# Delta rule of a two-block network: heads 2 and 3 with swapped chunk halves, 64-column blocks, passes of two head groups in turn

## The chip, the cores and the metric

The kernel runs on one core of one Trainium2 chip. The metric is the device time of one execution in microseconds (us), median of the runs shown. One core has TensorE (PE in the rows; PEld is its weight load), VectorE (DVE), ScalarE (ACT), GpSimd (POOL) and DMA queues that are issued from SyncE (SP) or from the other engines. TensorE multiplies a stationary operand (the weights, loaded by a LDWEIGHTS) with a moving one and writes to PSUM, which has eight banks of 128 partitions x 512 numbers in fp32.

## The reference

Two blocks of two layers each work on a sequence of 512 tokens of width 1024. The change lies in the second block's gated delta rule: four heads, key and value width 128, chunks of 64 tokens (eight chunks). Cut to what matters:

```
q, k, v, beta, g = chunk(q), chunk(k), chunk(v), chunk(beta), chunk(g)   # chunks of C = 64
g = cumsum(g)
decay = exp(where(tril, g_i - g_j, -inf))
A = where(strict, (k*beta) @ k.T * decay, 0)
T = inverse of (A + eye)                       # unit lower triangular, 64x64 for each chunk and head
u = T @ (v*beta);  w = T @ (k*beta*exp(g))
qk = (q @ k.T) * decay
for each chunk:                                # state S is 128x128 for each head
    v_new = u - w @ S
    o = (q*exp(g)) @ S + qk @ v_new
    S = S*exp(g_last) + (k*exp(g_last - g)).T @ v_new
```

Around it stand the input projections, a causal convolution of width 4 with silu over q, k, v, a dilated attention of eight heads, and the output projection. o is normalised and gated with silu(z).

## The kernel before

One program for the core. All projections are written as three fp32r matmuls for each k tile (`mm3`, lines 179 to 181: high x high, low x high, high x low parts), 512 columns wide; these are most of TensorE's work and serve as filler between the steps of everything else. A scheduler puts the instructions of all parts in one order for each engine by priority; `merges()` stands in a block of higher priority. Work in fp32 runs as two passes for each matmul, each pass a weight load and a stream.

The function `mix2` holds the delta rule. Tokens stand as four tiles of 128 rows (t = 0 to 3), each two chunks of 64 (u = 0, 1). The steps, with their lines:

- z, beta and gates (L915 to L955), the convolution and silu (`conv_silu`, L957 to L970), `k_rows` (transposes of k and its norms).
- Decays and scores for each head: `gB` by matmuls with 128 columns (L1011), `G` = k k.T (L1020), exps for each 128 columns (L1022, L1027), `A` (L1023). Each 128x128 tile holds two chunks, of which the off-diagonal quarters are masked to zero.
- The diagonal 16x16 blocks of A go through DRAM (`dA`), are solved on DVE and go back (`dT`). `q_rows` makes q k.T (L1060).
- `merges()`: for each head the inverse is merged from 16 to 32 to 64 rows: transposes (L274, tile `ps_d`), A x TT (L1120), a copy to X on ACT (L1122), T x X (L1125), a subtraction on DVE (L1126); then u (L1129), w (L1137), copies on ACT. The four heads follow one another in a pipeline.
- The scan, eight steps: `pv` = w S (L1151), `vn` = u + pv on DVE (L1152), `qv` = q S (L1154), `dS` = k.T vn (L1160), the new S on DVE (L1161). pv and qv fill 64 rows of their bank, dS reads 64 rows. After two steps `po` = qk vn (L1167) and the output's norm (L1164 to L1178).
- Attention (L1184 on): casts of its operands into the tiles of A, qT, kN and ET once these are free (L1189 to L1193), scores (L1219, L1220; tile `ps_s`), flips (`ps_pt`), values (L1237, `ps_o`), `delta_out` (flips of o, tile `ps_po`), and the projection (`ps_mo`).

PSUM banks are dealt by role (`deal`): a role with one bank waits until the former tile of that bank has been read.

Of the kernel before, what the change touches and what calls it, by code (L numbers as in the profile page):

```python
# [17 lines left out]
P = 128  # L18
# [19 lines left out]
def shape_consts():  # L38
# [5 lines left out]
    for d in (3, 2, 1, 0):  # L44
# [10 lines left out]
    m16 = (i // 32 == j // 32) & (i % 32 >= 16) & (j % 32 < 16)  # L55
    m32 = same & (i % 64 >= 32) & (j % 64 < 32)
# [3 lines left out]
        "mask_ls": np.where(same & (i > j), 0.0, NEG),  # L60
        "mask_u": np.where(same & (i <= j), 0.0, NEG),
# [29 lines left out]
def body(ctx, tc, a, out, plan, n1=LAYERS, n2=LAYERS, dbg=None):  # L91
# [759 lines left out]
    def rng2(i):  # L851
        return np.arange(o2[i], o2[i + 1])

    def z_w(l, j):
        return take_n("w_in_2", l, np.concatenate([rng2(6)[j * 256:j * 256 + 256], rng2(7 + j)]), range(KT))

    def block2(xt, xd, pss):
        with ExitStack() as c2:
# [15 lines left out]
            dA = [dr.tile([P, 4, SEQ], F32, name=f"dA{l}", bufs=1) for l in range(LAYERS)]  # L874
            dT = [dr.tile([P, 4, SEQ], F32, name=f"dT{l}", bufs=1) for l in range(LAYERS)]
            zt = tmp()
            nc.gpsimd.memset(zt, 0.0)
            for l in range(n2):
                for h in range(4):
                    nc.sync.dma_start(dT[l][:, h], zt)  # L880
# [5 lines left out]
    def mix2(l, rt, xt, par, row, dA, dT, pss):  # L886
# [3 lines left out]
        with ExitStack() as cm:  # L890
            pm = pool(f"pm{l}", cm)
            deal(mm=(0, 1, 2), tr=(3,), d=(4, 5, 6, 7), pv=(4,), qv=(5,), dS=(6,), po=(7,),
# [18 lines left out]

            d_gain, a_log, dt_b = row[:, 0:128], row[:, 128:132], row[:, 132:136]
# [7 lines left out]
            for j in range(2):  # L920
                def ev(t, ps, j=j):
                    zs = z[t][:, tsl(j, 256)]
                    silu2(ps[:, :256], zs, 256)
                    nc.vector.scalar_tensor_tensor(heads(zs, 2), heads(zs, 2), 0.5, mid(d_gain, 2), ALU.mult, ALU.mult)
                    nc.vector.tensor_copy((bb, aa)[j][:, :, t], ps[:, 256:260])
# [20 lines left out]
            nc.vector.tensor_tensor(graw, sp, end(ea, NT), ALU.mult)  # L946
            ps = bank("d")
            nc.tensor.matmul(ps[:, 0:16], cc("tri"), f16(graw), start=True, stop=True)
            nc.tensor.matmul(ps[:, 16:32], cc("same"), f16(graw), start=True, stop=True)
            gc, ngc, kd, eg = s16("gc"), s16("ngc"), s16("kd"), s16("eg")  # L950
            nc.vector.tensor_copy(f16(gc), ps[:, 0:16])
            nc.vector.tensor_scalar(f16(ngc), ps[:, 0:16], -1.0, None, ALU.mult)
            nc.vector.tensor_tensor(f16(kd), ps[:, 16:32], f16(gc), ALU.subtract)
            nc.scalar.activation(kd, kd, AF.Exp)
            nc.scalar.activation(eg, gc, AF.Exp)  # L955


            def conv_silu(m, ps, dst):
                with tc.high_priority(offset=0):
                    conv_silu_(m, ps, dst)  # L960

# [485 lines left out]
```

## Time and profile before

| | us |
|---|---|
| median of 3 runs | 2142.76 (2141.4 to 2145.73) |
| the profiled execution | 2143.14 |
| its span, first to last instruction | 2141.4 |
| around the span | 1.7 |
| TensorE busy in the span | 2059.3 (96%) |
| VectorE busy | 1261.0 (59%) |
| ScalarE busy | 959.2 (45%) |

A busy time is the sum over the records of an engine, and TensorE's passes overlap in their records, so a share of 96% doesn't say that the array is at its peak. The granted clock is 0.994 over the span. In layer 1 of the second block, the stretch 735 to 830 us holds decays, scores and the projections of q and v, 830 to 872 the merges, 872 to 916 the scan, 916 to 941 projections alone, 941 to 1012 the attention. Layer 2 repeats this at 1420 to 1760 us.

### The profile page before, as it was taken

The page shows a single profiled execution, that of the slowest core. Times are in us where ns is not written, and L with a number is a line of the kernel's source. Part 1 is how long each engine was busy: PE and PEld are TensorE (multiplying, and loading weights), DVE is VectorE, ACT ScalarE, POOL GpSimd, SP SyncE. Part 2 cuts the span into 40 slices and gives each one's busy share as a digit, 9 for nine tenths or more (in the row PEclk, how much of TensorE's full clock was granted, in tenths as well). Part 3 has the DMA queues.
Part 4 walks back from the last instruction along what each step waited for, and adds up shares of the span by engine and source line. Part 5 has one row for each costly group of instructions (what it writes and reads, how often), then busy time and mean ns, then how long its engine had stood idle before and what let it go on. Part 6 is the DMA issues. An engine that isn't in the chain of part 4 may idle for free.

```text
span 2141.4 us, 28239 instructions
## 1 busy us (share of the span) xinstructions
PE 2059.3 (96%) x10824; PEld 1709.0 (80%) x10824; DVE 1261.0 (59%) x2106; ACT 959.2 (45%) x1805; POOL 195.5 (9%) x337
## 2 busy tenths in 40 slices
PE   7899999999998899999999999999999999999998
PEld 6687878777887788778788888878887778888886
DVE  5667655667845676663666425577757446662364
ACT  4735444644534553255544324346333644442342
POOL 1110001110001111200200000021112010000001
PEclk9999999999999999999999999999999999999999
DMA  5232133322132522131533333243212144333332
GB/s 169 84 92 69 70 109 118 103 85 91 54 124 84 182 84 59 43 94 50 179 116 93 96 99 99 69 151 121 73 52 60 45 133 152 94 94 98 99 98 89
DMA packets 73717, 207.30 MB, mean 97 GB/s; under 512 B 16560, under 2 KB 17584, under 8 KB 73328
## 3 DMA queue, kind: packets, MB, share of 16 engines
q1 hardware_dynamic: 62576, 200.80, 30.3%
q10 hardware_dynamic: 11008, 4.72, 0.9%
q8 instruction: 85, 1.39, 0.3%
q14 instruction: 48, 0.39, 0.1%
HBM read 182.16 MB, written 17.04 MB: 93 GB/s over the span
## 4 chain that ended last, share of the span: by engine, by line
PE 76%; DVE 7%; ACT 6%; DMA 5%; issue 4%; POOL 3%; POOLq 0%; ACTq 0%; SPq 0%; DVEq 0%
PE ps_mm L180 18%; PE ps_mm L181 18%; PE ps_mm L179 18%; DMA wr<-in_w 4%; DVE wl L144 2%; PE ps_tr L274 2%; PE ps_o L1237 2%; ACT wh L143 2%; PE ps_pt L274 1%; PE ps_mo L181 1%; PE ps_mo L179 1%; PE ps_mo L180 1%; PE ps_s L1220 1%; POOL r2h L297 1%; ACT xn L296 1%
## 5 line engine op out<-in xcount | busy, mean ns | idle before, releaser
L144 DVE TENSOR_TENSOR wl<-wr,wh 128x1024 fp32r<-128x1024 f32 (+4 forms) x304 | 360.7, 1189 | 392.5 <-ACT wh L143 391.2
L143 ACT CAST wh<-wr 128x1024 fp32r<-128x1024 f32 (+4 forms) x304 | 309.3, 1019 | 354.7 <-PE ps_mm L181 151.2
L180 PE MATMUL ps_mm<-wl,xh 128*128 128x512 f32 (+2 forms) x736 | 283.4, 386 | 8.6 <-DVE wl L144 8.6
L181 PE MATMUL ps_mm<-x2h,wl 128*128 128x512 f32 (+1 forms) x768 | 285.9, 372 | 0.0
L179 PE MATMUL ps_mm<-x2h,wh 128*128 128x512 f32 (+1 forms) x768 | 285.7, 372 | 0.0
L180 PE MATMUL ps_mm<-x2l,wh 128*128 128x512 f32 (+1 forms) x768 | 285.7, 372 | 0.0
L179 PE MATMUL ps_mm<-wh,xh 128*128 128x512 f32 (+2 forms) x736 | 283.5, 387 | 1.9 <-ACT wh L143 1.8
L181 PE MATMUL ps_mm<-wh,xl 128*128 128x512 f32 (+2 forms) x736 | 281.7, 384 | 0.0
L180 PEld LDWEIGHTS ps_mm<-wl,xh 128*128 128x128 f32 x736 | 140.3, 191 | 37.2 <-DVE wl L144 14.8
L180 PEld LDWEIGHTS ps_mm<-x2l,wh 128*128 128x128 f32 x768 | 144.8, 189 | 25.0
L179 PEld LDWEIGHTS ps_mm<-x2h,wh 128*128 128x128 f32 x768 | 144.7, 188 | 24.9
L181 PEld LDWEIGHTS ps_mm<-x2h,wl 128*128 128x128 f32 x768 | 144.8, 188 | 24.8
L179 PEld LDWEIGHTS ps_mm<-wh,xh 128*128 128x128 f32 x736 | 139.8, 190 | 28.4 <-ACT wh L143 4.6
L181 PEld LDWEIGHTS ps_mm<-wh,xl 128*128 128x128 f32 x736 | 140.2, 191 | 23.3 <-issue 0.7
L1331 DVE SCALAR_TENSOR_TENSOR rt<-ps_mm,par,rt 128x511 f32<-128x511 f32 (+1 forms) x176 | 131.3, 746 | 4.8 <-ACT rt L1328 1.8
L179 PE MATMUL ps_mm<-xh,wh 128*128 128x512 f32 x320 | 128.0, 400 | 0.9 <-DVE rp L358 0.9
L181 PE MATMUL ps_mm<-xh,wl 128*128 128x512 f32 x320 | 127.1, 397 | 0.0
L180 PE MATMUL ps_mm<-xl,wh 128*128 128x512 f32 x320 | 127.0, 397 | 0.0
L297 POOL TENSOR_SCALAR r2h<-ss 128x1 f32<-128x1 f32 x48 | 19.4, 404 | 996.7 <-ACT th L296 759.8
L179 PE MATMUL ps_mm<-wh,hh 128*128 128x512 f32 x224 | 88.6, 397 | 0.3 <-ACT wh L143 0.2
L180 PE MATMUL ps_mm<-wl,hh 128*128 128x512 f32 x224 | 88.6, 397 | 0.1
L181 PE MATMUL ps_mm<-wh,hl 128*128 128x512 f32 x224 | 88.5, 397 | 0.0
(403 smaller groups left out, 3826.9 us busy)
## 6 DMA issues: line engine op xcount, KB each, us to landing
wr<-in_w SPq DMA_DIRECT2D x270, 512.0 KB, 3.6
gain<-in_gain SPq DMA_DIRECT2D x13, 512.0 KB, 6.4
wr<-in_w SPq DMA_DIRECT2D x14, 384.0 KB, 3.0
x<-in_x SPq DMA_DIRECT2D x8, 512.0 KB, 6.0
wm<-gqk SPq DMA_DIRECT2D x32, 128.0 KB, 2.4
xd<-x SPq DMA_DIRECT2D x8, 512.0 KB, 2.6
xs<-xd SPq DMA_DIRECT2D x8, 512.0 KB, 4.1
xs<-xm SPq DMA_DIRECT2D x8, 512.0 KB, 4.6
```

The source lines that it names most:

```text
L143: nc.scalar.copy(hi[:, :n], raw[:, :n])
L144: nc.vector.tensor_tensor(lo[:, :n], raw[:, :n], hi[:, :n].bitcast(F32), ALU.subtract)
L179: nc.tensor.matmul(ps, l[0], r[0], start=start, stop=False)
L180: nc.tensor.matmul(ps, l[0], r[1], start=False, stop=False)
L181: nc.tensor.matmul(ps, l[1], r[0], start=False, stop=stop)
L274: nc.tensor.transpose(ps[:w, tsl(j)], src[:, tsl(j, w)], ident)
L296: nc.scalar.activation(junk[i], halves[i], AF.Square, accum_out=ss[:, i:i + 1])
L297: nc.gpsimd.tensor_scalar(r[:, i:i + 1], ss[:, i:i + 1], 1.0 / D, r[:, 0:1] if i else EPS, ALU.mult, ALU.add)
L1220: nc.tensor.matmul(o_s, q_[own], kl[own, h // 2, :w], start=False, stop=True)
L1237: nc.tensor.matmul(o[:, tsl(h, 64)], p_[:, tsl(i * (qt + 1) + j)], av[:, j, tsl(h, 64)], start=j == 0, stop=j == qt)
L1331: nc.vector.scalar_tensor_tensor(acc[:, j:], ps[:, :SEQ - j], par[:, w0 + 3 * m + 2 - j:w0 + 3 * m + 3 - j], acc[:, j:], ALU.mult, ALU.add)
```

## The change

Heads 0 and 1 (group 0) stay as they are. Heads 2 and 3 (group 1) hold each pair of chunks in swapped halves: z, beta, the gates and the silu's results are written with chunk u in half 1 - u, and `delta_out` swaps back. So at one step of the scan group 0 works in one half of the partitions and group 1 in the other. Line numbers of the changed kernel are those of its own file.

- Decays (`M`, L1058 and L1060), scores (`G`, L1071) and q k.T (L1110) are made as 64x64 blocks, alternating between the two column halves of TensorE; A and E hold two heads in one 128x512 tile, so the exps and products go by 512 columns.
- The 16x16 blocks are written to DRAM twice, plain and transposed (`dT[0]`, `dT[1]`: 32 DMAs in place of 16 over both layers), which replaces the first transposes; `dA` is written by 4 DMAs in place of 8.
- The merges work on two heads at once, with 64x64 matmuls over 64 rows that alternate between the quadrants (0,0) and (64,64) and write to two banks (L1183, L1186); u (L1196) in the same quadrants, w (L1200) in row halves; transposes (L1179) with 64 rows.
- The scan issues the passes of the two groups in turn: pv and qv (both L1241) in alternating column halves, dS (L1253) in alternating row halves and two banks; vn and S are updated in two pieces of 256 columns. The norm of tile t - 1 (`delta_norm`, po at L1220) is issued after the first step of tile t. `vn` has three buffers.
- dS takes banks 6 and 7, and po moves to bank 3, which `tr` and the attention's `o` use as well.

Matmuls on TensorE over both layers: L1011's 32 become 128; L1020's and L1060's 32 each become 64 each; L1120's and L1125's 128 become 256; u's and w's 32 each become 64 each; transposes 64 become 32; eight small ones (L982) come in; 184 of pv, qv and dS stay 184.

The core of the diff:

```diff
-            deal(mm=(0, 1, 2), tr=(3,), d=(4, 5, 6, 7), pv=(4,), qv=(5,), dS=(6,), po=(7,),
+            deal(mm=(0, 1, 2), tr=(3,), d=(4, 5, 6, 7), pv=(4,), qv=(5,), dS=(6, 7), po=(3,),
                  s=(0, 1, 4), pt=(2, 5), o=(3,), mo=(6, 7))
...
+            F, B = slice(0, 64), slice(64, 128)
+            HF = (F, B)
...
+                if m % 4 < 2:
+                    nc.vector.scalar_tensor_tensor(dst, th, 1.0, acc, ALU.add, ALU.mult)
+                else:
+                    for u in range(2):
+                        nc.vector.scalar_tensor_tensor(chunks(dst)[:, :, 1 - u], chunks(th)[:, :, u], 1.0,
+                                                       chunks(acc)[:, :, u], ALU.add, ALU.mult)
...
+            tri = cc("tri")
+            for g in range(2):
+                M = bank("d")
+                for i in range(8):
+                    h, t, o = 2 * g + i // NT, i % NT, M[:, tsl(i, 64)]
+                    for p in HF:
+                        nc.tensor.matmul(o[p], ngraw[:, h, t:t + 1].to_broadcast([P, 64]), tri[:, p], start=True, stop=False)
+                    for p in HF:
+                        nc.tensor.matmul(o[p], tri[:, p], graw[:, h, t:t + 1].to_broadcast([P, 64]), start=False, stop=True)
                 d = dt()
+                nc.vector.tensor_tensor(b64(d), b64(M), mid(cc("mask_ls"), 8), ALU.add)
+                nc.vector.scalar_tensor_tensor(b64(E[:, g]), b64(M), -1.0, mid(cc("mask_u"), 8), ALU.mult, ALU.add)
                 flush()
+                nc.scalar.activation(d, d, AF.Exp)
+                nc.scalar.activation(E[:, g], E[:, g], AF.Exp)
                 G = bank("d")
+                for i in range(8):
+                    for p in HF:
+                        kc = chunks(kT[2 * g + i // NT])[:, i % NT, HF.index(p)]
+                        nc.tensor.matmul(G[p, tsl(i, 64)], kc, kc, start=True, stop=True)
+                nc.vector.tensor_tensor(d, d, G, ALU.mult)
+                nc.vector.tensor_tensor(b64(A[:, g]), b64(d), end(f16(sa[:, 2 * g:2 * g + 2]), 64), ALU.mult)
+                nc.scalar.dma_start(dA[:, 2 * g:2 * g + 2], A[:, g].rearrange("p (h c) -> p h c", h=2))
...
+            nc.vector.tensor_copy(Lb, Rb.rearrange("p r c -> p c r"))
             for u in range(8):
-                nc.scalar.dma_start(diag(dT, u), Rb[16 * u:16 * u + 16])
+                nc.scalar.dma_start(diag(dT[0], u), Rb[16 * u:16 * u + 16])
+                nc.scalar.dma_start(diag(dT[1], u), Lb[16 * u:16 * u + 16])
...
-                ps = bank("tr")
+                ps = bank("tr")[:, :256]
                 for t in range(NT):
-                    nc.tensor.matmul(ps[:, tsl(t)], kT[h][:, tsl(t)], qT[h][:, tsl(t)], start=True, stop=True)
-                nc.vector.tensor_tensor(ET[h], ps, ET[h], ALU.mult)
+                    for u, p in enumerate(HF):
+                        nc.tensor.matmul(ps[p, tsl(t, 64)], chunks(kT[h])[:, t, u], chunks(qT[h])[:, t, u],
+                                         start=True, stop=True)
...
+            def halves(f):
+                ps = bank("d"), bank("d")
+                for i in range(8):
+                    for p, b in zip(HF, ps):
+                        f(i, p, b)
+                return tuple(zip(HF, ps))
...
+                    T, TT = dt(), dt()
+                    for x, d in ((T, dT[0]), (TT, dT[1])):
+                        nc.scalar.dma_start(x.rearrange("p (h c) -> p h c", h=2), d[:, 2 * g:2 * g + 2])
+                    As = dt(), dt()
+                    for A_, m in zip(As, ("m16", "m32")):
+                        nc.gpsimd.tensor_tensor(b64(A_), b64(A[:, g]), mid(cc(m), 8), ALU.mult)
+                    for A_ in As:
+                        if A_ is As[1]:
+                            for j in range(2):
+                                ps = bank("d")
+                                for t in range(NT):
+                                    nc.tensor.transpose(ps[F, tsl(t)], TT[:, tsl(NT * j + t, 64)], ident)
+                                for u, p in enumerate(HF):
+                                    nc.scalar.copy(b64(T[p, tsl(j, 256)]), chunks(ps[F])[:, :, u])
+                        X = dt()
+                        for p, ps in halves(lambda i, p, b: nc.tensor.matmul(
+                                b[p, tsl(i, 64)], A_[p, tsl(i, 64)], TT[p, tsl(i, 64)], start=True, stop=True)):
+                            nc.scalar.copy(X[p], ps[p])
+                        for p, ps in halves(lambda i, p, b: nc.tensor.matmul(
+                                b[p, tsl(i, 64)], T[p, tsl(i, 64)], X[p, tsl(i, 64)], start=True, stop=True)):
+                            nc.vector.tensor_tensor(TT[p], TT[p], ps[p], ALU.subtract)
+                    Tk = dt()
+                    nc.vector.tensor_tensor(b64(Tk), b64(TT), end(f16(sk[:, 2 * g:2 * g + 2]), 64), ALU.mult)
+                    for j in range(2):
+                        h = 2 * g + j
+                        ps = bank("d"), bank("d")
                         for t in range(NT):
+                            for p, b in zip(HF, ps):
+                                nc.tensor.matmul(b[p, tsl(t)], TT[p, tsl(NT * j + t, 64)], vs[h][p, tsl(t)],
+                                                 start=True, stop=True)
+                        for p, b in zip(HF, ps):
+                            nc.scalar.copy(uN[p, :, tsl(h)], v4(b[p]))
+                    for u, (p, ps) in enumerate(halves(lambda i, p, b: nc.tensor.matmul(
+                            b[:, tsl(i, 64)], kN[2 * g + i // NT][p, tsl(i % NT)], Tk[p, tsl(i, 64)],
+                            start=True, stop=True))):
+                        for j in range(2):
+                            nc.scalar.activation(chunks(wT_[:, 2 * g + j])[:, :, u], b64(ps[:, tsl(j, 256)]), AF.Copy,
+                                                 scale=-1.0)
+                    for h in (2 * g, 2 * g + 1):
+                        nc.vector.tensor_tensor(v4(kN[h]), v4(kN[h]), end(kd[:, h], P), ALU.mult)
...
+                order = [(g, 2 * g + j) for j in range(2) for g in range(2)]
+                vns = []
+                def delta_norm(t):
+                    oN = uN[:, t]
...
+                for t in range(NT):
+                    vn = gt("vn", 3)
+                    qv = bank("qv")
+                    for u in range(2):
+                        pv = bank("pv")
+                        for x, ps in ((wT_, pv), (None, qv)):
+                            for g, h in order:
+                                xh = qT[h] if x is None else x[:, h]
+                                nc.tensor.matmul(ps[HF[u ^ g], tsl(h)], chunks(xh)[:, t, u ^ g], S[:, h],
+                                                 start=True, stop=True)
+                            if x is not None:
+                                for g in range(2):
+                                    p, c = HF[u ^ g], tsl(g, 256)
+                                    nc.vector.tensor_tensor(vn[p, c], uN[p, t, c], pv[p, c], ALU.add)
+                        if 2 * t + u < 7:
+                            S_ = pm.tile([P, 4, P], F32, tag="S", name="S", bufs=3)
+                            nc.gpsimd.tensor_tensor(S_, S, end(decl[:, :, t, u], P), ALU.mult)
+                            dS = bank("dS"), bank("dS")
+                            for g, h in order:
+                                p = HF[u ^ g]
+                                nc.tensor.matmul(dS[g][:, tsl(h % 2)], kN[h][p, tsl(t)], vn[p, tsl(h)], start=True, stop=True)
+                            for g in range(2):
+                                Sg = S_[:, 2 * g:2 * g + 2]
+                                nc.vector.tensor_tensor(Sg, Sg, heads(dS[g][:, :256], 2), ALU.add)
+                            S = S_
+                        if u == 0 and t:
+                            delta_norm(t - 1)
+                    nc.vector.tensor_tensor(v4(uN[:, t]), v4(qv), end(eg[:, :, t], P), ALU.mult)
+                    vns.append(vn)
+                delta_norm(NT - 1)
```

Three places of TensorE's order in layer 1, each of before and then of the changed kernel. Rows of `ps_mm` are the projections' mm3.

The merges, at one head's second merge before, from its transposes (L274 on `ps_d`) to u and w:

```order
L1125 MATMUL ps_d<-dt 128x128 x4
L181 MATMUL ps_mm<-wh,xl 128x512
...
L274 MATMUL ps_d<-ident,dt 128x128 x4
L1120 MATMUL ps_d<-dt 128x128 x4
L179 MATMUL ps_mm<-wh,xh 128x512
...
L1125 MATMUL ps_d<-dt 128x128 x4
L180 MATMUL ps_mm<-wl,xh 128x512
...
L1129 MATMUL ps_d<-vs,dt 128x128 x4
L1137 MATMUL ps_d<-dt 128x128 x4
```

The same in the changed kernel for the second group (two heads):

```order
L1183 MATMUL ps_d<-dt 64x64 x16
L182 MATMUL ps_mm<-wl,xh 128x512
...
L1186 MATMUL ps_d<-dt 64x64 x16
L276 MATMUL ps_tr<-ident,cv 128x128 x2
...
L1183 MATMUL ps_d<-dt 64x64 x4
L1179 MATMUL ps_d<-ident,dt 64x128 x8
L1183 MATMUL ps_d<-dt 64x64 x12
L276 MATMUL ps_tr<-ident,cv 128x128 x4
...
L1186 MATMUL ps_d<-dt 64x64 x16
```

Four heads with about four mm3 matmuls between dependent groups have become two groups of heads, with one to six other rows between their steps; each group is now a group of small tiles.

The scan, one step before (pv, qv, then dS of two neighbouring steps):

```order
L1151 MATMUL ps_pv<-S,A 64x128 x4
L1154 MATMUL ps_qv<-S,qT 64x128 x4
L1160 MATMUL ps_dS<-vn,kN 128x128 x4
L180 MATMUL ps_mm<-wl,xh 128x512
...
L1151 MATMUL ps_pv<-S,A 64x128 x4
L1154 MATMUL ps_qv<-S,qT 64x128 x4
```

The same in the changed kernel:

```order
L1241 MATMUL ps_pv<-S,A 64x128
L1241 MATMUL ps_qv<-S,qT 64x128
L183 MATMUL ps_mm<-wh,xl 128x512
L181 MATMUL ps_mm<-wh,xh 128x512
L1241 MATMUL ps_pv<-S,A 64x128 x3
L1241 MATMUL ps_qv<-S,qT 64x128 x3
L182 MATMUL ps_mm<-wl,xh 128x512
L1253 MATMUL ps_dS<-vn,kN 128x128 x4
```

Groups of four have been cut into one and three, with mm3 between. Over one layer of `mix2`, TensorE goes from full-size tiles into half or quarter tiles 13 times in the order before and 47 times in the changed one (attention's scores left out of both), and changes between two small shapes 3 and 7 times.

The end of the scan and the start of the attention, before:

```order
L1154 MATMUL ps_qv<-S,qT 64x128 x4
...
L1167 MATMUL ps_po<-vn,ET 128x128 x4
...
L274 MATMUL ps_tr<-ident,cv 128x128 x4
...
L1219 MATMUL ps_s<-kN,A 128x256 x3
...
L1237 MATMUL ps_o<-av,cv 128x64 x2
...
L274 MATMUL ps_po<-ident,kT 128x128 x4
L1237 MATMUL ps_o<-av,cv 128x64 x2
```

The same in the changed kernel:

```order
L276 MATMUL ps_tr<-ident,cv 128x128 x4
...
L1253 MATMUL ps_dS<-vn,kN 128x128 x4
...
L1220 MATMUL ps_po<-vn,ET 128x128 x2
...
L1305 MATMUL ps_s<-kN,A 128x256 x3
...
L1323 MATMUL ps_o<-av,cv 128x64
...
L276 MATMUL ps_po<-ident,uN 128x128 x4
...
L1323 MATMUL ps_o<-av,cv 128x64 x16
```

The last steps of the scan now come after the last flips of the projections (`ps_tr`). Between the last po and the first scores there were 111 mm3 matmuls (with two `ps_tr` flips); now there are 37. All four flips of delta_out (`ps_po`) now stand ahead of the values (`ps_o`) of the second query tile, 16 in one row.

## Rows read from the trace of the kernel before

**Rows 1.** The page: the span, and busy time of each engine.
```profile
span 2141.4 us, 28239 instructions
...
PE 2059.3 (96%) x10824; PEld 1709.0 (80%) x10824; DVE 1261.0 (59%) x2106; ACT 959.2 (45%) x1805; POOL 195.5 (9%) x337
```
**Rows 2.** Windows, layer 1: stretch, length, busy (count) of each engine, clock, DMA.
```profile
735.00:830.00 95.00, 92.08 (x487) 77.32 (x488) 71.15 (x153) 49.45 (x118) 13.17 (x19) 1.00 0.32 96
830.00:872.00 42.00, 39.97 (x278) 34.26 (x277) 24.63 (x34) 18.18 (x37) 8.29 (x6) 1.00 0.24 70
872.00:916.00 44.00, 42.61 (x286) 34.66 (x286) 25.98 (x47) 6.33 (x11) 11.03 (x12) 1.00 0.00 1
916.00:941.00 25.00, 25.00 (x119) 20.62 (x118) 20.20 (x22) 12.83 (x13) 1.20 (x2) 1.00 0.47 127
941.00:1012.00 71.00, 71.00 (x428) 55.80 (x427) 28.36 (x85) 40.75 (x106) 0.19 (x1) 1.00 0.22 63
```
**Rows 3.** Waits of PE, 690 to 1012 us: us in total, times, longest.
```profile
PE ps_d L1129 <- DVE dt L1126: 1.8, 1, 1.8
PE ps_pv L1151 <- DVE S L1161: 1.4, 2, 0.8
```
**Rows 4.** Timeline of PE, one group of the merges: start, us, instruction.
```profile
856.29 1.06 PE L1120 MATMUL ps_d<-dt 128*128 128x128 f32 x8
857.10 0.48 PE L181 MATMUL ps_mm<-wh,xl 128*128 128x512 f32 x1
```
**Rows 5.** Timeline, one step of the scan.
```profile
875.74 0.40 PE L181 MATMUL ps_mm<-wh,xl 128*128 128x512 f32 x1
875.97 0.39 PE L179 MATMUL ps_mm<-wh,xh 128*128 128x512 f32 x1
876.29 1.09 PE L1151 MATMUL ps_pv<-S,A 128*64 128x128 f32 x8
877.31 0.50 PE L180 MATMUL ps_mm<-wl,xh 128*128 128x512 f32 x1
```
**Rows 6.** Timeline of PE in block 1, row halves in turn (second and last pair of eight).
```profile
81.86 0.27 PE L547 MATMUL ps_sf<-wm 64*128 64x128 f32 x1
81.87 0.27 PE L547 MATMUL ps_sb<-wm 64*128 64x128 f32 x1
...
82.53 0.27 PE L547 MATMUL ps_sf<-wm 64*128 64x128 f32 x1
82.54 0.27 PE L547 MATMUL ps_sb<-wm 64*128 64x128 f32 x1
```
**Rows 7.** Timeline of PE in block 1, column halves in turn, and the instruction after.
```profile
118.61 1.09 PE L587 MATMUL ps_og<-S,wm 128*64 128x128 f32 x16
119.64 0.50 PE L179 MATMUL ps_mm<-wh,xh 128*128 128x512 f32 x1
```
**Rows 8.** Groups of weight loads, 830 to 916 us: count, busy, mean ns.
```profile
L1154 PEld LDWEIGHTS ps_qv<-S,qT 128*64 128x64 f32 x64 | 7.2, 137 | 0.1
...
L1120 PEld LDWEIGHTS ps_d<-dt 128*128 128x128 f32 x56 | 6.8, 192 | 1.2 <-issue 1.2
```
**Rows 9.** Timeline of PE, attention's values (64 columns moved, 128 of weights).
```profile
1004.78 3.68 PE L1237 MATMUL ps_o<-av,cv 128*128 128x64 f32 x32
1008.27 0.47 PE L179 MATMUL ps_mo<-wh,xh 128*128 128x512 f32 x1
```
**Rows 10.** Groups of DVE, 735 to 916 us: count, busy, mean ns, idle before.
```profile
L1126 DVE TENSOR_TENSOR dt<-dt,ps_d 128x512 f32<-128x512 f32 x8 | 5.5, 684 | 10.6 <-PE ps_d L1125 10.6
...
L357 DVE TENSOR_TENSOR th<-ps_mm,cs 128x256 f32<-128x256 f32 x12 | 4.7, 415 | 0.0
...
L1193 DVE TENSOR_TENSOR A<-aqT,A 64x2048 fp32r<-64x2048 f32 x1 | 2.3, 2285 | 0.0
```
**Rows 11.** Groups of ACT, 735 to 916 us.
```profile
L1122 ACT COPY dt<-ps_d 128x512 f32<-128x512 f32 x8 | 4.7, 587 | 4.5 <-PE ps_d L1120 4.5
...
L1192 ACT CAST A<-aqT 64x2048 fp32r<-64x2048 f32 x1 | 1.9, 1902 | 4.3 <-PE ps_pv L1151 4.3
```

More of the change, by code (lines that the diff above doesn't have):

```diff
@@ L59, in shape_consts @@
         "same": same,
-        "mask_ls": np.where(same & (i > j), 0.0, NEG),
-        "mask_u": np.where(same & (i <= j), 0.0, NEG),
+        "mask_ls": np.where(ib > jb, 0.0, NEG),
+        "mask_u": np.where(ib <= jb, 0.0, NEG),
         "m16": m16,
@@ L854, in z_w @@
     def z_w(l, j):
-        return take_n("w_in_2", l, np.concatenate([rng2(6)[j * 256:j * 256 + 256], rng2(7 + j)]), range(KT))
+        two_ = [rng2(i)[2 * j:2 * j + 2] for i in (7, 8)]
+        return take_n("w_in_2", l, np.concatenate([rng2(6)[j * 256:j * 256 + 256], *two_]), range(KT))
     def block2(xt, xd, pss):
@@ L872, in block2 @@
                 row.append(r_)
-            dA = [dr.tile([P, 4, SEQ], F32, name=f"dA{l}", bufs=1) for l in range(LAYERS)]
-            dT = [dr.tile([P, 4, SEQ], F32, name=f"dT{l}", bufs=1) for l in range(LAYERS)]
+            dA = [dr.tile([P, 4, 256], F32, name=f"dA{l}", bufs=1) for l in range(LAYERS)]
+            dT = [[dr.tile([P, 4, 256], F32, name=f"dT{l}{i}", bufs=1) for i in range(2)] for l in range(LAYERS)]
             zt = tmp()
@@ L878, in block2 @@
             for l in range(n2):
-                for h in range(4):
-                    nc.sync.dma_start(dT[l][:, h], zt)
+                for d in dT[l]:
+                    for g in range(2):
+                        nc.sync.dma_start(d[:, 2 * g:2 * g + 2], zt.rearrange("p (h c) -> p h c", h=2))
             for l in range(n2):
@@ L984, in rows @@
                 return [ap[:, i] for i in range(4)]
-            A, ET, kN, qT = rows(set4("A")), rows(set4("ET")), rows(set4("kN")), rows(set4("qT"))
-            kT = [gt("kT", 4) for _ in range(4)]
+            wT_, ET_, kN, qT = set4("A"), set4("ET"), rows(set4("kN")), rows(set4("qT"))
+            nc.gpsimd.memset(ET_, 0.0)
+            kT = rows(set4("kT"))
+            A = pm.tile([P, 2, SEQ], F32, name="A")
+            E = pm.tile([P, 2, SEQ], F32, name="E")
             ssk, ssq = s16("ssk"), s16("ssq")
@@ L1004, in mix2 @@
                 late.append(lambda h=h: k_rows(h))
-            decl = pm.tile([P, 4, 8], F32, name="decl")
-            for h in range(4):
-                gB = bank("d")
-                for t in range(NT):
-                    nc.tensor.matmul(gB[:, tsl(t)], graw[:, h, t:t + 1].to_broadcast([P, P]), cc("tri"),
-                                     start=True, stop=True)
-                nc.scalar.activation(decl[:, h], gB.rearrange("p (n c) -> p n c", c=64)[:, :, 63], AF.Exp)
+            tri = cc("tri")
```

133 lines of the change are left out of this document (49 added, 84 removed).

## The prediction

> **What bounds the kernel now.** The page comes first: TensorE's records cover 2059 of 2141 us of the span, no other engine passes 60% [rows 1]. So the question is where TensorE's time goes and what lets it wait. The windows of layer 1's mixing answer for the stages that change: merges 40.0 of 42 us busy, scan 42.6 of 44, attention 71 of 71 [rows 2]; their sum with the other two stretches is 270.7 of 277. The list of waits names what lies in the gaps, a few steps of the chain of merges and scan [rows 3]. The steps of the delta rule are thus already filled by the projections' mm3, and a step that becomes shorter on another engine gains little. What can gain is TensorE's own work, so it is counted in start-to-start times, not busy times (records overlap).
>
> **Price of one pass.** Eight fp32 passes of the merges take 0.81 us to the next mm3 [rows 4], 32 passes of the values 3.49 us, 0.109 each [rows 9]: 0.11 us a pass. The values move only 64 columns and cost the same, for their weights have 128 columns. The load of 64 columns of weights lasts 137 ns, that of 128 columns 192 [rows 8], 55 ns less. A pass with 64 columns on both sides stands in no row. Its lower bound is half of 0.11, 0.055 us; its upper bound is 0.11, no gain. Two passes in different halves do run side by side: in block 1 the second to the last of eight row-half pairs, six intervals, take 0.67 us, 0.112 a pair, and the two of a pair start 0.01 us apart [rows 6]; 16 passes in alternating column halves take 1.03 us to the next mm3 [rows 7], 0.13 a pair with all edges. So a pair costs what one pass costs. For pairs with 64 columns on both sides I take 0.055, as both ingredients (half the load, pairs side by side) have a row.
>
> The Trainium skill, in "TensorE: Matmul & The Clock Gate", section "The mechanism" of Part 3, speaks against this for column halves: a weight load runs beside another tile's matmul only if the two are in different row groups, and two column halves share theirs. By that rule the pairs of decays, scores, q k.T, pv and qv would pay the second load, at 0.055 us for 384 such pairs 21 us more than the sum below, 2162 us. The column halves of block 1 don't bear it out: 16 passes one behind the other would take 1.76 us and take 1.03 [rows 7].
>
> **The passes, both layers** (matmuls x 2 passes x 0.11, then pairs). Scores: 32 matmuls, 7.0 us, become 64 pairs at 0.055, 3.5: -3.5. q k.T the same: -3.5. Inverse: 128 matmuls, 28.2 us, become 256 pairs at 0.055, 14.1: -14.1. Transposes: 32 fewer single passes: -3.5. Decays: 32 matmuls, 7.0 us, become 128 pairs at 0.055: 0. u and w: 32 matmuls each become 64 pairs each with 128 columns on one side, at 0.11: 0. pv, qv, dS: 184 matmuls, 368 passes, 40.5 us, become 184 pairs at 0.11: -20.2. Eight small matmuls for the decay of the last row, 16 passes: +1.8. Sum -43.0 us.
>
> **Lost pairs.** The passes pair up only if the order lets them. I walked down the changed order with one rule: a pass starts once the pass of its own half is over and the pass ahead of it in the order has started. Groups cut by an mm3 leave odd pieces: in the scan's step shown, the single pv and qv lie in one half, and each piece of three has two of its matmuls in one half; eight matmuls take 12 pass times of 0.11 in place of 8, where before they took 16. Such pieces cost 8 us in all over both layers; the two passes of a matmul, which stand behind each other in one half and hold up the other half's, cost 7.5 more: +15.5.
>
> **Changes of shape.** Before the first pass of pv the mm3 takes 0.32 us in place of 0.23, and the eight passes take 1.02 to the next mm3, where eight full-size passes take 0.81 [rows 4, 5]: 0.09 + 0.21 = 0.30 us for one trip into small tiles. The order has 47 trips a layer in place of 13: 34 x 2 x 0.30 = 20.4 us. Four more changes between two small shapes a layer, taken at half a trip: 1.2. Together +21.6.
>
> So TensorE's own work: -43.0 + 15.5 + 21.6 = **-5.9 us**. The gain of the pairs is all but eaten by pieces and trips.
>
> **Waits.** Merges: a group's chain is four groups of passes (each 32 passes, 16 pairs at 0.055, with a trip 1.2 us), two copies to X in halves (each 2 x 0.587), two subtractions in halves (2 x 0.684, both [rows 10, 11]), four quarter copies of T at no more than 0.587 and one product of 0.68: near 13 us with no handover counted, against 21 us for each half of the 42 before. The same wait is taken as before, 2 us of idle a layer [rows 2], and 0 for the sum; between -2 and +3 a layer. Handing over halves costs DVE little: vn and S in two pieces are 2 x 0.415 in place of 0.684 [rows 10], 0.15 us later a step, behind the mm3 of that step.
>
> Start of the attention: between the last po and the first scores there were 111 mm3, 25 us [rows 2], and now 37, at 0.227 us 8.4 us. DVE has to make the low parts of four operand tiles, 2.285 us each [rows 10], and the five operations of the last norm, about 0.68 each: 12.5 us, of which two tiles (A and kN) come free before the last po. ACT's four casts, 1.9 each [rows 11], go beside. What shows is between 0 and 12.5 - 8.4 = 4.1; I take 1.5 a layer, +3.
>
> Values behind delta_out: po and o share bank 3, so the second tile's 16 value matmuls wait for four flips, each with a cast and a subtraction (0.587 and 0.684) before the bank is free: 4 x (0.44 + 1.27) = 6.8 us, beside which the order places 22 mm3 (5 us), scores and flips. Between 0 and 3 a layer; I take 0.5, +1.
>
> The other edits cost nothing on the path: sixteen more dT DMAs are issued on ACT, which loses 64 short exps over both layers and is 42% busy in the merges (18.2 of 42 us); the split z, gates and silu pieces lie on DVE, 75% busy (71.2 of 95 us) beside a TensorE that is full in that stretch [rows 2]. If that cover were gone, the silu's two pieces are 0.15 us each.
>
> Sum: -5.9 + 0 + 3 + 1 = **-1.9 us** on the profiled execution's 2143.1 (span 2141.4 and 1.7 around it), which is 0.4 above the median: **2141 us**. A measurement of this kernel can tell 0.2%, 4.3 us, from no change.
>
> **Rivals.** *Faster:* the trips overlap with waits that are there anyway, and pairs that the walk counts as lost are made up because a weight load can run ahead. Then the 15.5 halves and a fifth of the trips is free: -1.9 - 7.8 - 4.3 = -14, 2129 us. For it speaks that 2.0 and 1.4 us a layer stand idle in merges and scan, just where the trips are made [rows 2]; against it that the 0.30 was read from a full stream.
>
> *Slower:* a pair of 64-column passes doesn't reach 0.055. Four instructions in 0.055 us are 73 a us, and the densest row, the pairs of block 1, has four in 0.112, 36 a us [rows 6]. There are 512 such pairs (128 decays, 128 scores, 256 inverse); each ns above 55 costs 0.5 us, so from 67 ns on the kernel is slower than before by over 4.3 us, and at 0.11 it is 28 us slower: 2169. Of the chance for this rival, 0.05 is for column pairs that pay both loads: their 384 pairs cost 0.055 us more each, 21 us, 2162. (The rule of the Trainium skill's "TensorE: Matmul & The Clock Gate", "The mechanism", would have it so.)
>
> *Slower in another place:* DVE's work ahead of the first scores and the flips on bank 3 show in full: 2 x (4.1 + 3) in place of 4, +10: 2151 us.
>
> *The change doesn't do what it says:* the passes in turn run one behind the other. The rows of block 1 exclude it for 128 columns; no chance of its own.
>
> **How the numbers follow.** The forecast has 0.40, with a range of its own of 2135 to 2147; the faster rival 0.25; the 64-column pairs 0.22; the late attention 0.13. The range from 2124 to 2162 leaves out one in ten at the top (pairs above 95 ns) and as much at the bottom. Faster by over 0.2%: 0.25 and a third of the forecast, 0.38. Within: half of the forecast and a few hundredths of each other case, 0.27. Slower: the rest, 0.35.
>
> **What would show it.** In the changed profile: the 16-matmul rows of the inverse near 0.9 us to the next mm3 (1.8 and more if pairs don't reach 0.055); pv and qv starts in pairs 0.01 us apart; mm3 ahead of each small-tile group at 0.32; the stretch from merges to scan's end shorter, that of the attention longer; PE waits on `kN`, `vs` or `A` before the first scores. It would be wrong if pairs cost over 67 ns, or if a wait of more than 4 us a layer stood at one of the named places.

## The result, and the profile after

The changed kernel takes 2169.32 us (median of four runs, 2160.37 to 2177.48) against 2142.08 for the kernel before (2138.37 to 2145.73): a ratio of 1.0119, 95% interval 1.0086 to 1.0153. It is slower by 27 us, where the prediction had 2141 and a range up to 2162.

The page of the changed kernel, its span, busy times, and the row of the clock over 40 slices of the span:

```profile
span 2170.5 us, 29618 instructions
...
PE 2085.8 (96%) x11512; PEld 1708.8 (79%) x11512; DVE 1260.6 (58%) x2178; ACT 946.9 (44%) x1751; POOL 194.9 (9%) x331
...
PEclk9999999999999999987999999999899899999999
```

TensorE's busy time grew by 27 us [rows 1], VectorE's and ScalarE's didn't. The last row tells why: slices 18, 19 and some later ones are below 9. The mean granted clock fell from 0.994 to 0.978. The windows of layer 1 (columns as in [rows 2]; the clock is the third number from the right) show where:

```profile
735.00:812.00 77.00, 75.22 (x565) 60.72 (x564) 52.69 (x123) 35.34 (x78) 15.97 (x19) 1.00 0.32 92
812.00:850.00 38.00, 34.76 (x430) 28.70 (x431) 23.91 (x35) 18.28 (x36) 2.82 (x2) 0.91 0.17 57
850.00:929.00 79.00, 77.35 (x463) 57.05 (x461) 45.04 (x85) 21.62 (x27) 9.56 (x11) 1.00 0.21 64
938.00:1012.00 74.00, 71.86 (x302) 55.87 (x303) 31.98 (x90) 35.20 (x101) 3.48 (x3) 0.72 0.09 29
```

The attention (938 to 1012 us) ran at a mean clock of 0.72, where the stretch of [rows 2] had 1.00, and TensorE counts as busy through nearly all of it. In finer windows:

```profile
944.00:948.00 4.00, 2.96 (x13) 1.76 (x12) 3.78 (x10) 1.37 (x6) 0.00 (x0) 1.00 0.00 0
948.00:952.00 4.00, 3.85 (x18) 2.62 (x17) 2.26 (x10) 2.76 (x11) 0.00 (x0) 0.80 0.59 167
952.00:956.00 4.00, 4.00 (x12) 2.38 (x11) 0.85 (x5) 1.32 (x7) 0.00 (x0) 0.50 0.26 99
...
968.00:972.00 4.00, 4.00 (x20) 2.70 (x21) 3.57 (x12) 3.27 (x10) 0.00 (x0) 1.00 0.17 69
980.00:984.00 4.00, 4.00 (x11) 1.68 (x10) 2.25 (x8) 2.39 (x8) 0.19 (x1) 1.00 0.02 4
984.00:988.00 4.00, 4.00 (x21) 3.89 (x21) 0.00 (x0) 0.96 (x2) 0.00 (x0) 0.57 0.00 0
...
1004.00:1008.00 4.00, 4.00 (x22) 4.00 (x21) 0.00 (x0) 1.88 (x4) 0.00 (x0) 0.50 0.00 0
```

A clock of 0.50 is 1.2 GHz, 1.00 is 2.4. It falls twice, from about 950 to 968 and from 984 to 1010 us. What TensorE did ahead of it: the first time two waits of 1.1 and 1.0 us with twenty mm3 between them, and then scores, flips and values with hardly an mm3; the second time 24 mm3 among flips (971.7 to 980 us), ten scores of 384 or 512 columns in a row, with no wait at all, and then 32 value passes. The price of the low clock stands in the timeline, to be read beside [rows 9], where 32 such passes in a row took 3.49 us at a full clock:

```profile
984.11 6.70 PE L1323 MATMUL ps_o<-av,cv 128*128 128x64 f32 x32
990.60 0.85 PE L276 MATMUL ps_pt<-ident,dt 128*128 128x128 f32 x3
```

They took 6.49. The same passes cost nearly double.

**A measure.** In each window of 2 us, 2 us x (1 - granted clock) is the time lost to the clock, if TensorE sets the pace there; summed over the span (whole windows only, which leaves out up to 0.8 us at its end) I call it the lost clock. It is 11.1 us in the kernel before and 46.6 in the changed one, 35.5 more. The span less the lost clock is 2130.3 before and 2123.9 after: 6.4 us less. Of the 46.6, 20.5 lie in layer 1's attention, 6.7 in layer 2's (1694 to 1708 us), 3.4 and 6.8 at the start of the merges (814 to 822, 1554 to 1570); the rest is about what the kernel before has too. The four runs bear the measure out to within 5 us: spans of 2170.5, 2164.6, 2158.6 and 2175.7 us had mean clocks of 0.978, 0.983, 0.985 and 0.977; span x clock is 2123, 2128, 2126 and 2126. It takes off too much where TensorE doesn't set the pace in a low stretch: over the eleven runs of a_sp2 below, span x clock goes from 2117 us at a clock of 0.986 to 2108 at 0.977. Differences of a few us between two kernels with much lost clock are thus not to be read from it.

The waits of TensorE, 690 to 1060 us, to be read beside [rows 3]:

```profile
PE ps_mm L181 <- DVE cv L1003: 3.9, 1, 3.9
PE ps_s L1305 <- DVE ss L1226: 1.1, 1, 1.1
PE ps_s L1305 <- DVE mx L1309: 1.0, 1, 1.0
```

The waits of [rows 3] are gone or short; a new one of 3.9 us stands ahead of the merges, and layer 2 has it too (3.7).

### The profile page after: what moved, and what is told of

It is laid out like the page before. It is cut to its first block, busy times and chain, and to the rows that moved or that the text cites. A ratio compares the mean times of both kernels' runs of the same rounds, so it can differ in the third digit from the quotient of the medians.

```text
span 2170.5 us, 29618 instructions
## 1 busy us (share of the span) xinstructions
PE 2085.8 (96%) x11512; PEld 1708.8 (79%) x11512; DVE 1260.6 (58%) x2178; ACT 946.9 (44%) x1751; POOL 194.9 (9%) x331
## 4 chain that ended last, share of the span: by engine, by line
PE 44%; DVE 2%; POOL 1%; ACT 1%; issue 1%; DMA 1%; POOLq 0%; DVEq 0%; ACTq 0%; SPq 0%
PE ps_mm L182 12%; PE ps_mm L181 12%; PE ps_mm L183 12%; PE ps_o L1323 1%; DMA wr<-in_w 1%; PE ps_tr L276 1%; PE ps_pt L276 1%; PE ps_s L1306 1%; POOL r2h L299 0%; DVE wl L146 0%; PE ps_s L1305 0%; PE ps_mo L181 0%; PE ps_d L1183 0%; PE ps_mo L183 0%; PE ps_mo L182 0%
```

## The experiments

Two causes were in question for the clock: that po's move to **bank 3** takes away the attention's mm3 and puts its values late, or that the **small tiles** themselves take the clock down. All ratios are to the kernel before, run together with each group of versions (medians 2142.2 to 2144.3).

**1. delta_out's flips back on bank 7 (a_out7).**

```diff
-            ... dS=(6, 7), po=(3,),
+            ... dS=(6, 7), po=(3,), out=(7,),
-                ps = flip(oN[:, t], role="po")
+                ps = flip(oN[:, t], role="out")
```

> The changed kernel with one thing undone: the flips of delta_out write to bank 7, which the projection uses too, in place of bank 3, which the attention's values use; po of the scan stays on bank 3. Theory (the order that bank 3 forces takes the clock down in the attention): the values go back between the scores, the low-clock stretch that came with the 32 value passes in one row (984 to 1008 us of the changed profile, 12 us lost in layer 1) goes away in part or in full, the stretch at 950 to 966 us may stay, since the 37 mm3 ahead of the first scores stay 37. Time 2150 to 2162 us. Rival (the passes in small tiles take the clock down, wherever po stands): clock mean stays at 0.978, time 2165 to 2172.

Measured 2157.23 us, 1.0066 (1.0041 to 1.0091). The values stand between the scores again, and layer 1's attention ran at a full clock; layer 2's did not:

```profile
946.00:1010.00 64.00, 63.98 (x391) 50.07 (x390) 27.39 (x86) 37.82 (x105) 0.19 (x1) 1.00 0.15 47
1664.00:1704.00 40.00, 40.00 (x139) 29.77 (x139) 15.77 (x56) 17.84 (x57) 0.00 (x0) 0.53 0.16 53
```

The same order in both layers, once at 1.00 and once at 0.53 for 40 us: this version stands at an edge. Nearly half of the loss is back (12 of 27 us), and the cause isn't the late values alone. The waits of 1.1 and 1.0 us ahead of the scores are here too, and layer 1 kept its full clock behind them, so these waits alone don't take it down.

**2. po on bank 7 throughout (a_po7).**

```diff
-            ... dS=(6, 7), po=(3,),
+            ... dS=(6, 7), po=(7,),
```

> The changed kernel with po on bank 7 throughout, in the scan and in delta_out; dS keeps banks 6 and 7. The last steps of the scan then come before the last flips of the projections, and 128 mm3 in place of 37 stand between the last po and the first scores. Theory (bank 3): no low-clock stretch in the attention, mean clock near 0.99, time 2133 to 2143 us, that is the 6 us of less work of TensorE that the changed profile shows beside its lost clock; po and dS on one bank may cost 1 to 3 us of waits in the scan. Rival (small tiles): clock 0.98, time 2160 to 2172.

Measured 2142.9 us, 1.0005 (0.9991 to 1.0019): the 27 us are gone. The attention of layer 1 is at 1.00:

```profile
938.00:1012.00 74.00, 74.00 (x438) 58.10 (x439) 29.48 (x92) 41.72 (x114) 0.19 (x1) 1.00 0.11 34
```

The lost clock of the profiled run, 5 us above the median, is 22.6 us, of which 8.5 still lie at the start of the two merges. Span less lost clock is 2124.0, the same as the changed kernel's 2123.9: by this measure the bank moved only the clock.

**3 and 4. The kernel before with po on bank 3 (b_po3), and with delta_out's flips alone on bank 3 (b_out3).**

```diff
-            ... dS=(6,), po=(7,),
+            ... dS=(6,), po=(3,),              # b_po3
+            ... dS=(6,), po=(7,), out=(3,),    # b_out3, and delta_out's flip with role="out"
```

> The kernel before with one thing of the change: po on bank 3 in place of 7, in the scan and in delta_out. No small tile is added. Theory (bank 3): the attention loses its cover as in the changed kernel (24 mm3 in place of over 100 ahead of the first scores), the granted clock falls to half there, time 2150 to 2170 us. Rival (small tiles): clock stays 0.99, time within 2138 to 2147 us, a few us of waits at most.

> The kernel before with delta_out's flips alone on bank 3; po of the scan stays on bank 7. The values of the second query tile come behind the four flips, the mm3 ahead of the first scores stay over 100. Theory (bank 3, and of its two effects the late values): a low-clock stretch about where the values stand in rows, 3 to 10 us lost over both layers, time 2145 to 2155 us. If only the cover ahead of the scores counts: 2139 to 2146 us. Rival (small tiles): 2138 to 2146 us.

b_po3 takes 2162.69 us, 1.011 (1.0083 to 1.0136), with not one small tile more. Its windows:

```profile
940.00:950.00 10.00, 9.44 (x43) 6.91 (x42) 8.31 (x19) 5.17 (x15) 2.04 (x2) 1.00 0.17 55
950.00:974.00 24.00, 23.25 (x75) 15.86 (x74) 10.66 (x38) 12.46 (x37) 0.00 (x0) 0.50 0.22 66
974.00:1000.00 26.00, 26.00 (x172) 20.85 (x169) 8.92 (x25) 15.48 (x40) 0.19 (x1) 1.00 0.01 2
```

Its longest wait in the attention is 0.6 us, its lost clock 31.6 us, 20.5 more than the kernel before, and it is 20 us slower. b_out3 takes 2145.83, 1.0011 (0.9998 to 1.0024), with no low clock in the attention: there 103 mm3 stand between the last po and the first scores, as in the kernel before, in b_po3 24. (The 111 named ahead of the result have eight passes of `ps_tr` flips among them; the trace of the kernel before has 103 mm3 and these eight.) So one line of the change, the bank of po, makes the loss in a kernel that has nothing else of it, and small tiles aren't needed for it. The flips of delta_out on bank 3 don't make it by themselves; whether the scan's po alone would make all of it in the kernel before, no run shows (in the changed kernel, a_out7, it made a little over half).

**5 to 7. The queue of the dT writes, on top of a_po7.** ScalarE's timeline in the changed kernel at the new wait (ACTq are issues of DMAs; the third number is their time):

```profile
799.95 0.31 ACTq L1096 DMA_DIRECT2D dT<-dt  x1
800.30 0.46 ACTq L1095 DMA_DIRECT2D dT<-dt  x1
...
810.53 0.46 ACTq L1096 DMA_DIRECT2D dT<-dt  x1
811.04 0.69 ACT L1001 ACTIVATE cv<-ps_mm,half_w 128x512 f32<-128x512 f32 x1 [11.11 <-DMA dT<-dt]
```

For 11 us ScalarE does nothing but issue fifteen of its sixteen writes, with a pause of 2.8 us in the middle (804.7 to 807.5) whose cause isn't shown; a convolution waits behind them, DVE waits for it, and TensorE's mm3 waits for the bank that DVE has to read. The kernel before had eight writes in 4.81 us there:

```profile
814.86 4.81 ACTq L1047 DMA_DIRECT2D dT<-dt  x8
```

```diff
-                nc.scalar.dma_start(diag(dT[1], u), Lb[16 * u:16 * u + 16])
+                nc.sync.dma_start(diag(dT[1], u), Lb[16 * u:16 * u + 16])     # a_po7_sp
+                nc.gpsimd.dma_start(diag(dT[1], u), Lb[16 * u:16 * u + 16])   # a_po7_pool
-                nc.scalar.dma_start(diag(dT[0], u), Rb[16 * u:16 * u + 16])
+                nc.sync.dma_start(diag(dT[0], u), Rb[16 * u:16 * u + 16])     # a_po7_sp2, besides the first
```

> The variant with po on bank 7, with the eight transposed dT writes of each layer issued on SyncE's queue in place of ScalarE's. In that variant's trace ScalarE issues 16 dT writes from 803.5 to 814.7 us and runs nothing else (8 writes, 4.8 us before the change), the projection waits 4.1 us for DVE behind it, and the clock falls for 8 us (3.4 us lost); layer 2 has the same wait, 3.6 us. Theory (the doubled writes on ScalarE's queue are what the changed kernel still pays at that place): the wait goes, the fall of the clock with it, 4 to 7 us a layer: 2129 to 2136 us. Rival (the diagonal solve and the landing of the writes set the start of the merges, whoever issues them): the wait moves to the merges' first matmul, time 2139 to 2146.

> The same variant with all sixteen dT writes of a layer on SyncE's queue. Theory (ScalarE's queue): ScalarE is free at that place, 2127 to 2135 us; weight loads on SyncE's queue come up to 8 us later there and may give some of it back. Rival (the landing sets it): 2139 to 2146.

> The same variant with the eight transposed dT writes of each layer on GpSimd's queue, which has little to do there. Theory (ScalarE's queue): like the one on SyncE, 2129 to 2136 us. Rival (the landing sets it): 2139 to 2146.

On SyncE the wait goes and the fall of the clock with it: 2134.5 us, 0.9958 (0.9941 to 0.9974), for half of the writes, 2126.33, 0.9928 (0.9912 to 0.9944), for all, lost clock 13.8 and 12.1. On GpSimd nothing is gained: 2142.8, 1.0 (0.9988 to 1.0011). There the eight writes take from 803.3 to 813.1 us, and the wait moves to the merges' first matmul, as the rival had it:

```profile
803.30 1.89 POOL L1096 DMA_DIRECT2D dT<-dt  x3 [2.09 <-DVE dt L1093]
...
812.57 0.57 POOL L1096 DMA_DIRECT2D dT<-dt  x1 [1.36 <-issue]
...
PE ps_d L1183 <- DMA dt<-dT: 5.0, 1, 5.0
```

So both the issuing engine and the end of the writes count. SyncE's queue takes all sixteen from 799.0 to 809.9 us in a_po7_sp2, and there no wait over 1.0 us is left between 798 and 1012 us.

**8. Passes one group behind the other (a_po7_seq).**

```diff
-                order = [(g, 2 * g + j) for j in range(2) for g in range(2)]
+                order = [(g, 2 * g + j) for g in range(2) for j in range(2)]
...
-                for i in range(8):
-                    for p, b in zip(HF, ps):
+                for p, b in zip(HF, ps):
+                    for i in range(8):
                         f(i, p, b)
```

The loop over u's matmuls is turned in the same way.

> The variant with po on bank 7, with the passes of the two groups one group behind the other in place of in turn: in the scan, the inverse and u and w all matmuls of the one half stand ahead of all of the other; nothing else moves. It prices the passes in turn by themselves. If pairs run side by side as priced in the prediction (128-column pairs at 0.11, 64-column pairs near 0.06 to 0.07 us): 184 pairs of the scan and 64 of u at 0.11 and 256 of the inverse at 0.06, less what the order cuts, would be lost: 20 to 35 us more of TensorE's work, 2160 to 2180 us. If a pair costs hardly less than its two passes: within 2140 to 2148.

Measured 2166.37 us, 1.0113 (1.0087 to 1.0138), within the range, but by another way than expected. In the profiled run, the longest of the five (2178.3 us), the lost clock is 45.1 us, 22.5 more than a_po7's, and span less lost clock is 2131.4, 7.4 more. In the other four span x clock is 2136 to 2139, where a_po7's ten runs have 2123 to 2126. So by this measure about 7 us are work in the profiled run and 13 in the others, and the rest is the clock. After the wait ahead of the merges 10.2 us are lost (816 to 838) where a_po7 loses 3.4, and in layer 2 22.2 (1548 to 1616) where a_po7 loses 5.1. At a full clock, an inverse's group (32 passes, sixteen in each half) and a scan's group (8), with the mm3 after each:

```profile
857.41 1.90 PE L1186 MATMUL ps_d<-dt 64*64 64x64 f32 x32
859.24 0.50 PE L181 MATMUL ps_mm<-wh,xh 128*128 128x512 f32 x1
...
867.43 0.66 PE L1241 MATMUL ps_pv<-S,A 128*64 128x128 f32 x8
868.03 0.50 PE L181 MATMUL ps_mm<-wh,xh 128*128 128x512 f32 x1
```

The changed kernel, with the passes in turn:

```profile
835.92 1.15 PE L1183 MATMUL ps_d<-dt 64*64 64x64 f32 x32
837.00 0.50 PE L182 MATMUL ps_mm<-wl,xh 128*128 128x512 f32 x1
837.88 1.60 PE L1186 MATMUL ps_d<-dt 64*64 64x64 f32 x32
839.41 0.44 PE L276 MATMUL ps_tr<-ident,cv 128*128 128x128 f32 x2
...
852.82 0.66 PE L1241 MATMUL ps_pv<-S,A 128*64 128x128 f32 x8
853.41 0.50 PE L181 MATMUL ps_mm<-wh,xh 128*128 128x512 f32 x1
```

The inverse's 32 passes take 1.08 us in turn and 1.82 one half behind the other (L1183); those of the second kind (L1186) take 1.24 to 1.61 in the changed kernel, where the records show them only in part side by side, and 1.83 here. The scan's eight take 0.59 in turn and 0.60 behind each other (0.96 in one group, at 883.7 us): four passes of one half don't hold up the four of the other. The starts in the records tell how far this goes. In an inverse's group here thirteen passes start one by one, 0.058 us apart; beside the thirteenth the first pair begins, and after a few pairs the rest start one by one again. As I read it (the records don't name the half), the second half starts beside the fourth pass from the end of the first; a scan's group has only four in a half, and its passes start in pairs 0.013 us apart.

**9 to 11. What the tiles are worth, on one chip (b_sp, a_po7_sp2 again, a_sp2).** b_sp is the kernel before, a_sp2 the changed kernel, each with only `nc.scalar.dma_start(diag(dT...` turned into `nc.sync`.

> The kernel before with its eight dT writes a layer on SyncE's queue. If the gain of the variant with po on bank 7 and all writes on SyncE (2126 us) comes from the queue alone, whatever the tiles: 2124 to 2131 us. If it comes from the tiles once the queue and the bank are mended: 2137 to 2145, since ScalarE's 4.8 us of writes held no wait of TensorE there in the kernel before.

> The same kernel as the variant with po on bank 7 and all dT writes on SyncE, beside the other two of this call on one chip: 2125 to 2132 us again.

> The changed kernel (po on bank 3) with all dT writes on SyncE's queue. Theory (the two causes add): the wait ahead of the merges and its low clock go, the low clock of the attention stays: 2148 to 2160 us. Rival (the attention's clock falls as a late effect of the first wait): 2126 to 2140.

b_sp: 2147.8 us, 1.0025 (1.0013 to 1.0036), a little slower: the queue alone gives nothing. a_po7_sp2 again: 2131.97, 0.9952 (0.9936 to 0.9968). a_sp2: 2148.76, 1.0033 (1.0014 to 1.0051), lost clock 29.2, most of it in the attentions:

```profile
946.00:962.00 16.00, 16.00 (x55) 11.23 (x56) 6.99 (x28) 8.93 (x31) 0.00 (x0) 0.57 0.19 61
1664.00:1690.00 26.00, 25.94 (x82) 17.71 (x83) 12.39 (x43) 14.07 (x45) 0.00 (x0) 0.54 0.19 61
```

The wait ahead of the merges is gone here, so it isn't what takes the attention's clock down. The version with both mends is the fastest one made, 0.5 to 0.7% under the kernel before.

**12. Work that is thrown away (a_fill).** The changed kernel as it stands, with two matmuls of 512 columns in each unit of the attention whose result nothing reads:

```diff
                 nc.scalar.copy(p_[:, :n], flip(e, n // P, role="pt")[:, :n])
+                fill = bank("mo")
+                for k in range(2):
+                    nc.tensor.matmul(fill, qe[:, 0, tsl(0)], ke[:, 0, :], start=k == 0, stop=k == 1)
                 return p_
```

> The changed kernel (po on bank 3, all dT writes on ScalarE) with 96 matmuls more: each of the attention's 24 units of a layer has two extra matmuls of 512 columns whose result nothing reads; they stand between its flips, scores and values, which stay in their late order. At 0.227 us each they are 11 us a layer, 22 us in all, of work that is thrown away. Theory (the attention of the changed kernel lacks wide matmuls between its small ones, and that takes the clock down): the two low-clock stretches of each layer's attention go or shrink, 25 to 35 us come back, so the 22 us cost nothing: 2155 to 2170 us, mean clock 0.988 or more. Rival (the late order itself or its waits cost the time): clock near 0.978 and time 2185 to 2195.

Measured 2163.04 us, 1.0095 (1.008 to 1.011), beside the changed kernel's 1.0119 (1.0086 to 1.0153): 22 us of added work cost no time. That the kernel became faster by it isn't shown, since the intervals overlap. The lost clock is 13.9 us in place of 46.6; no low stretch is left in either attention, and the 32 value passes still stand in a row:

```profile
946.00:966.00 20.00, 20.00 (x105) 14.22 (x104) 12.02 (x45) 14.53 (x47) 0.00 (x0) 1.00 0.25 79
980.00:1010.00 30.00, 30.00 (x197) 24.65 (x195) 7.70 (x19) 13.28 (x30) 0.00 (x0) 1.00 0.00 1
...
979.69 3.68 PE L1326 MATMUL ps_o<-av,cv 128*128 128x64 f32 x32
983.20 0.50 PE L276 MATMUL ps_pt<-ident,dt 128*128 128x128 f32 x3
```

Span less lost clock is 2147.4, the changed kernel's 2123.9 and 23.5. The 36 mm3 ahead of the first scores and waits of 1.4 and 0.6 us there are about the changed kernel's; what is new is the 512-column matmuls among scores, flips and values, and with them the clock stayed at 1.00. So the late order and its waits don't take the clock down as long as such matmuls stand among the small instructions, and the price of po's bank is the clock. The ten scores in a row are broken up too, so the fill doesn't tell which of the small instructions takes it down.

## Why the prediction was wrong

**The step that failed** is that on the start of the attention, and the one on the values behind delta_out. Both saw the right places: 37 mm3 in place of 103, and values late behind bank 3. Both priced them as waits, 3 and 1 us over both layers, at a full clock. In sum the waits were about that, 2.1 us a layer, but all of it stands ahead of the scores (1.1 and 1.0 us); at the values no wait over 0.2 us shows. But every pass price of the sum was read at a clock of 1.00, and nothing in the sum asked what holds the clock there. Once the cover was gone the clock fell in the attention, 27.2 us lost over both layers (20.5 and 6.7). b_po3 makes the loss without the rest of the change, a_po7 takes it away, a_fill does too by added work. The Trainium skill ("TensorE: Matmul & The Clock Gate", "What's actually happening") says that the clock is set by how busy the array has lately been; the traces agree as far as waits go (814 us: a wait of 3.9 us, then 0.50), and show more: at 984 us it fell with no idle time in the rows.

**The second failed step** is the sentence that the dT writes cost nothing. I counted their number and ScalarE's share, not that they stand in one piece: 11 us in which ScalarE's queue runs nothing. It costs waits of 3.9 and 3.7 us and the clock behind them, 3.4 and 6.8 us lost in this trace. Moving the writes takes 11 to 17 us off a_po7 (2142.9 to 2126.3 and 2132.0), where the same move in the kernel before gains nothing (b_sp).

**TensorE's work, -5.9 us.** Span less lost clock fell by 6.4, which looks like a hit, but holds the two new waits of 7.6 us. Without them (a_po7_sp2) it is 2117.5, 12.8 less than before. Of these, 4.5 are idle time: span less busy time was 82.1 us before [rows 1] and is 77.6 in a_po7_sp2:

```profile
PE 2052.0 (96%) x11512; PEld 1683.3 (79%) x11512; DVE 1261.7 (59%) x2178; ACT 947.7 (45%) x1751; POOL 193.0 (9%) x331
```

Busy time less lost clock is 2048.2 before, 2039.2 in the changed kernel, 2039.5 in a_po7 and 2039.9 in a_po7_sp2. So TensorE's work shrank by 8 to 9 us, and the sum was 2 to 3 too small, which is about what this measure can tell.

Of its terms, the pair of 64-column passes holds. In quadrants sixteen pairs with their trip took 1.08 us, and 16 x 0.055 and 0.30 are 1.18. In column halves, where neighbours have the same shape, sixteen pairs took 0.93, 0.058 each:

```profile
753.89 1.10 PE L1071 MATMUL ps_d<-kT 128*64 128x64 f32 x32
754.82 0.29 PE L1058 MATMUL ps_d<-cst,ngraw 128*64 128x64 f32 x4
```

That it holds is in part luck. The prediction says that half the load has a row, but that row has 137 ns beside 192 [rows 8]; half the time for a pass was only its lower bound, and a_po7_seq's 32 passes in 1.83 us (0.057 each, nearly all one by one) are the first rows that show it.

The shape changes hold for the scan: the mm3 ahead of pv takes 0.32 or 0.33. The 8 us of odd pieces hold where the scan is cut: single pv and qv took 0.58 us to the next mm3, three of each 1.02 (856.83 to 857.85), 4 and 8 pass times and the edges:

```profile
855.59 0.43 PE L1241 MATMUL ps_pv<-S,A 128*64 128x128 f32 x2
855.86 0.38 PE L1241 MATMUL ps_qv<-S,qT 128*64 128x128 f32 x2
856.17 0.50 PE L182 MATMUL ps_mm<-wl,xh 128*128 128x512 f32 x1
```

The lost pairs were oversized in one part: the 7.5 us for passes held up by the pass ahead of them show nowhere in the scan. By the walk a whole group of eight would take five pass times, and it takes 0.59 us, four and the edges; a_po7_seq has the same with four passes of one half ahead of the other's. In groups of sixteen a half they do cost. On the other side the inverse's second kind isn't fully side by side: its eight groups take 2.3 us more in a_po7_sp2 than eight of 1.08. The other terms weren't priced one by one, so that the total came near is in part errors that cancel.

**The rivals.** That of the 64-column pairs gave 2169 us, and the kernel came to 2169, by luck and another way: the pairs run at their price. The one on the attention had the place and the sign, and a price of 10 us where it cost 27. The faster rival was right that passes counted as lost aren't, where no more than four stand in a half. The rule of the Trainium skill ("TensorE: Matmul & The Clock Gate", "The mechanism") on the weight loads of column halves isn't borne out: pv's four pairs take 0.59 us with all edges, where eight passes in one half took 1.02 [rows 5].

**Left open:** what exactly in the small passes lets the clock fall (few columns, weight loads, half of the rows in the second matmul of each score; 32 value passes in a row don't by themselves, [rows 9] and a_fill), why a_out7's two layers differ, and why the clock comes back later when the merges' passes stand one half behind the other. The kernels show that it is so, not why.

## What to carry to other kernels

Read the granted clock of each stretch beside its busy time, and before an edit moves the filler of a stage with many small matmuls, ask what will hold the clock there: here a bank shared by two roles moved 79 of 103 filler matmuls away from its start (b_po3). When a change makes a kernel slower, take the lost clock off first; here that led to two causes of a line or two each, and without them the same change is 10 to 16 us faster than the kernel before where with them it is 27 us slower. A run of DMA issues on an engine that also computes is a wait as long as the run, however idle that engine is on the whole.

## What the runs showed of the hardware

TensorE's clock fell to half while its rows show it busy 4.00 of 4 us, with no wait ahead (984 us), and 96 matmuls that nobody reads kept it up: 22 us of added work at no cost in time. Pairs of 64-column passes run at 0.058 us a pair in column halves, and sixteen pairs in quadrants take 1.08 us with all edges. Passes need not alternate one by one to run side by side: four against four cost 0.60 us in place of 0.59, sixteen passes against sixteen 1.82 in place of 1.08. Eight small DMA writes that GpSimd's queue issued took 9.8 us, fifteen on ScalarE's 11.0 during which ScalarE computed nothing, and sixteen on SyncE's 10.9.
